# Written order on TensorE in the in-projection stage of a hybrid decoder step

## The chip, the cores and the metric

The kernel runs on one core of a Trainium2 chip. The metric is device time in microseconds, from one launch to its end; the time of a kernel is the median over its runs. PE is TensorE, DVE VectorE, ACT ScalarE, POOL GpSimd, SP SyncE.

## The reference, cut to what matters

One inference step of two trunk layers for 1024 prompt tokens and 64 sample tokens (8 requests of 8), all in float32. The stage that is changed is the in-projection of layer 0 and what follows it directly:

```
proj = x @ w_in                          # 1088 tokens, 1024 -> 2816
a = conformer_conv(proj[:, :512], proj[:, 512:1024])    # gate, 31 taps
xm = proj[:, 1024:] + mu * (prev - proj[:, 1024:])      # token shift
r, k, v, dw, da, dg = split(xm)
wlog  = -softplus(-(w0 + tanh(dw) @ w2)) - 0.5
decay = exp(-exp(wlog)) ;  a = sigmoid(a0 + da @ a2)
kk = k * k_k ;  kk = kk / max(sqrt(sum(kk * kk, head)), 1e-12)
kf = k * (1 + (a - 1) * k_a)
o, S = rwkv_scan(r, kf, v, decay, -kk, kk * a, state)   # 8 heads of 64
bonus = sum(r * kf * r_k, head) * v
```

The scan is computed in chunks of 64 tokens with masked products A of keys against queries and the inverse of a unit triangular matrix per chunk and head. After it come an output projection, a layer norm, a SwiGLU FFN, then layer 1 (pooling mixer and FFN).

## The kernel before, in words

Products in float32 are split in two parts each (`hl`, `xh`, `xl`), so each output tile of 128 features takes three products for each of the 8 slices k of the input. `proj` makes one tile: for three token blocks (384, 384, 320 tokens) 24 products into one psum buffer of the tag `mm` (two buffers), and then `evict`, which moves the block out on ACT and DVE. There are 22 tiles; `ORDER` gives their sequence:

```
ORDER = ("c0", "c1", 20, 21, 16, 12, 8, "c2", 17, 13, 9, "c3", 18, 14, 10, 19, 15, 11)
```

"c" tiles are the convolution (`conv_tile`: two tiles each, gate and value, and behind them 31 taps on DVE at line 319, of low priority, four small products on POOL and sums on DVE). 20 and 21 feed the small low-rank products. 16 + p, 12 + p and 8 + p are v, k and r of head pair p (`mix_tile`), p = 0 to 3.

`prep(p, blk, k)` prepares head pair p for token block blk. It is a Python generator: it issues its instructions up to a `yield`, and goes on at the next `next`. In order it makes: on PE the two low-rank products `pz` and `pa` (psum tag `o`, two buffers); tanh, scan `L`, exponentials `Wp` and `Wi`; on PE the sums of squares `pss` (psum tag `ch`); maximum `ri` on DVE (line 582), power on POOL (line 583), copy `exv` on ACT (line 586); on PE its transpose back (line 588) as a broadcast; `kn` on DVE (line 590), tanh `ta` on ACT (line 592), and on POOL `AR`, `kn`, `kf` and two parts of `BK` (lines 568 to 602). First `yield`. Then `AR` for r and the masked products `pA` on PE, two psum buffers for each of the two heads (tag `tp`, two buffers in all; `mm` for the last pair), which DVE masks into `ATm` (line 622), and the DMAs of all this to DRAM on SP's queue. Second `yield`. Then the bonus `pbn` and `bv`. `invert` inverts the diagonal blocks of a pair with 31 times two dependent instructions (lines 678 and 680), on POOL for pair 0 and the second part of pair 3, on DVE for the others. It loads its input back from DRAM.

Work is put on the engines by a planner: it takes instructions in the order of the program as priority, but plays the program through with modelled durations and gives each engine whatever is ready first. So the order of the queues of PE, ACT, DVE, POOL and SP around this stage is the planner's. From the second phase on (`phase2`, after the first part of the convolution's layer norm), `manual_schedule` takes that away for PE: PE's queue there is in the order in which the program is written.

After tile 12 + p the kernel before issues the first part of blocks 0 and 1, after tile 8 + p the second part of block 0, then block 2, block 1, block 2, the inversion and the third parts. With priority in program order these steps stand ahead of the tiles that follow.

Of the kernel before, what the change touches and what calls it, by code (L numbers as in the profile page):

```python
# [60 lines left out]
class Prog:  # L61
# [115 lines left out]

    GAP2 = 2.0

    _u = 0  # L180
    LATE = 2000
    CONV0 = 8
# [43 lines left out]
    def phase1(self):  # L226
        tc, nc, I, O = self.tc, self.nc, self.I, self.O
# [11 lines left out]
        es = ExitStack()  # L239
# [26 lines left out]
        def proj(m, evict):  # L266
            hl = first.pop(m, None) or self.load_w(I["w_in"][m].rearrange("p k f -> p (k f)"), f"in{m}")
            w = hl.rearrange("p s (k f) -> p s k f", k=KT)
            for b, (n0, n) in enumerate(NBLK):
                ps = self.psum("mm", f"in{m}_{b}")  # L270
                xh, xl = xb[b]
                for k in range(KT):
                    self.mm(ps[:, :n], w[:, 0, k, :], xh[:, k, :], k == 0, False)
                    self.mm(ps[:, :n], w[:, 0, k, :], xl[:, k, :], False, False)
                    self.mm(ps[:, :n], w[:, 1, k, :], xh[:, k, :], False, k == KT - 1)
                evict(b, n0, n, ps)

        self.accd = self.dr.tile([4, 128, TOK], F32, name="accd")
        def conv_tile(ct):
# [18 lines left out]
            def ev_val(b, n0, n, ps):  # L298
                for o, x in parts(n0, n, ps):
                    nc.vector.scalar_tensor_tensor(out=o, in0=o, scalar=1.0, in1=x, op0=ALU.add, op1=ALU.mult)  # L300

            proj(4 + ct, ev_gate)
            proj(ct, ev_val)
            nco = cvp.tile([128, (1 + NS) * CB], F32, tag="nco", name=f"nco{ct}")
            nc.scalar.activation(out=nco[:, 0:CB], in_=u[:, SEQ:SEQ + CB], func=AF.Copy, scale=0.5)
# [26 lines left out]
        def mix_tile(m):  # L332
# [16 lines left out]
            def ev(b, n0, n, ps):  # L349
# [5 lines left out]
                if p < n:  # L355
# [3 lines left out]
                                                   op0=ALU.mult, op1=ALU.add)  # L359

            proj(m, ev)
            sh = self.small.tile([128, 1 + NS], F32, tag="sho", name=f"sho{m}")
            nc.gpsimd.tensor_copy(out=sh[:, 0:1], in_=raw[:, SEQ:SEQ + 1])
# [7 lines left out]
            else:  # L371
                self.xm[m] = xm

        self.xm, done = {}, set()
        for x in self.ORDER:
            if isinstance(x, str):
                conv_tile(int(x[1]))
                continue
            mix_tile(x)
            done.add(x)  # L380
            p = x % 4
            if 16 <= x < 20:
                nc.scalar.dma_start(out=self.vd[p], in_=self.xm[x])
            elif 12 <= x < 16:
                jobs = [self.prep(p, blk, self.xm[x]) for blk in range(3)]
                next(jobs[0])
                next(jobs[1])
            elif 8 <= x < 12:
                next(jobs[0])
                if p == self.last_p:  # L390
                    self.invert(p, self.ip, 0, 6)
                for i in (2, 1, 2):
                    next(jobs[i])
                self.invert(p, self.ip, 6 if p == self.last_p else 0)
            if x in (16 + p, 8 + p) and {16 + p, 8 + p} <= done:
                for j in jobs:
                    next(j, None)
        es.close()


# [120 lines left out]
    def prep(self, p, blk, k):  # L521
# [9 lines left out]
        k = k[:, n0:n0 + n]  # L531
# [34 lines left out]
        def withW(out, in0, lo):  # L566

            nc.gpsimd.tensor_tensor(out=out[:, :cp], in0=ch(in0)[:, :cp], in1=Wv[:, :, lo:lo + 64], op=ALU.mult)
            if samp:
                nc.gpsimd.tensor_tensor(out=out[:, cp].rearrange("p (s l) -> p s l", l=8),  # L570
                                        in0=in0[:, np_:].rearrange("p (s l) -> p s l", l=8),
                                        in1=Ws[:, :, lo:lo + 8], op=ALU.mult)


        pss = self.psum("ch", f"pss_{nm}")
        prb = pss[:, 0:n]
# [7 lines left out]
        exv = self.tpool.tile([128, 6, 64], F32, tag="t", name=f"exv_{nm}")  # L584
        for a, b, m in ([(0, 6, 128)] if not samp else [(0, 4, 128), (4, 6, 64)]):
            nc.scalar.activation(out=exv[:m, a:b], in_=ri2[:m, a:b].unsqueeze(2).to_broadcast([m, b - a, 64]), func=AF.Copy, scale=-1.0)
        for i, (t0, m) in enumerate(TG):
            nc.tensor.transpose(prb[:, t0 - n0:t0 - n0 + m], exv[:m, 2 * i:2 * i + 2].rearrange("p a b -> p (a b)"), self.ident[:m, :m])
        kn = T("kn")
# [1163 lines left out]
```

## Time and profile before

| | us |
|---|---|
| median of 2 runs | 2301.02 (2300.99 to 2301.05) |
| the profiled execution | 2299.71 |
| its span, first to last instruction | 2297.9 |
| mean granted clock of TensorE, 1 is full speed | 0.953 |
| in-projection from its first product to its last | 7.5 to 401.3 |

The page of the profile gives for each engine the time in which it was busy. The span is that of the one core. A wait is told as the idle time of an engine before an instruction, with the instruction of another engine that ended it.

### The profile page before, as it was taken

The numbers are of one execution on the slowest core, as the hardware profiler recorded it, in microseconds if no ns is written. First come the engines' busy times: TensorE is split into PE (matmuls) and PEld (weight loads), VectorE is DVE, ScalarE is ACT, GpSimd is POOL, SyncE is SP. The second block draws the span as 40 slices with busy tenths as digits, with TensorE's granted clock in tenths as the row PEclk, the third lists the DMA queues.
The fourth block names the chain that finished last, engine by engine and source line by source line (L and its number), as shares of the span: only waits on it lengthen the run. The fifth ranks groups of instructions, "written<-read, shape, count | busy, mean of one in ns | idle before, by whom it ended". The sixth has DMA issues, their size and how long they took to land.

```text
span 2297.9 us, 39974 instructions
## 1 busy us (share of the span) xinstructions
PE 2148.6 (94%) x14794; PEld 1931.0 (84%) x14794; DVE 1672.4 (73%) x3115; ACT 906.4 (39%) x2031; POOL 445.6 (19%) x551
## 2 busy tenths in 40 slices
PE   8988899689888899999999999999999999999997
PEld 7887788467664699999998787879999999987876
DVE  6997798944457554888887767765388888877677
ACT  3242334545442543333333444443443333334452
POOL 3588966553421000000000001000000000000002
PEclk9999899598898899999999999999999999999999
DMA  5132334864541665666667785464386666678764
GB/s 171 42 104 91 109 89 132 235 187 117 159 133 57 215 236 196 224 222 221 221 211 255 255 281 174 140 197 146 133 284 224 228 220 222 204 261 274 241 195 136
DMA packets 286542, 427.68 MB, mean 186 GB/s; under 512 B 85484, under 2 KB 147844, under 8 KB 286339
## 3 DMA queue, kind: packets, MB, share of 16 engines
q1 hardware_dynamic: 209869, 318.44, 44.5%
q10 hardware_dynamic: 76478, 106.68, 13.2%
q8 instruction: 116, 1.90, 0.4%
q14 instruction: 79, 0.65, 0.1%
HBM read 296.14 MB, written 129.11 MB: 185 GB/s over the span
## 4 chain that ended last, share of the span: by engine, by line
PE 58%; DVE 6%; DMA 4%; issue 2%; ACT 2%; POOL 0%; SPq 0%; ACTq 0%; POOLq 0%; DVEq 0%
PE dn L74 14%; PE pp L74 1%; PE dr L74 1%; PE wo L74 1%; PE pl L74 1%; DMA yr<-yd 1%; ACT xo L155 1%; PE pa_1u L74 1%; PE pa_2u L74 1%; PE pa_4u L74 1%; PE pa_3g L74 1%; PE pa_5u L74 1%; PE pa_4g L74 1%; PE pa_2g L74 1%; PE pa_3u L74 1%
## 5 line engine op out<-in xcount | busy, mean ns | idle before, releaser
L74 PE MATMUL dn<-op_d,op_h 128*128 128x512 f32 x1848 | 452.6, 398 | 7.3 <-DVE yr L1297 3.7
L74 PEld LDWEIGHTS dn<-op_d,op_h 128*128 128x128 f32 x1848 | 346.0, 190 | 88.8 <-DVE yr L1297 5.2
L74 PE MATMUL in<-xh,hl_in 128*128 128x384 f32 (+1 forms) x1056 | 282.1, 348 | 15.9 <-ACT xh L71 7.5
L103 POOL TENSOR_TENSOR rstd_f<-rs_f,mhalf 128x1 f32<-128x1 f32 (+1 forms) x18 | 31.6, 1759 | 1343.1 <-DVE rs_f L102 689.6
L74 PEld LDWEIGHTS in<-xh,hl_in 128*128 128x128 f32 x1056 | 197.9, 199 | 29.2 <-ACT xm L352 7.8
L319 DVE SCALAR_TENSOR_TENSOR acc<-u,hv,acc 128x1024 f32<-128x1024 f32 x120 | 194.8, 1633 | 0.8
L74 PE MATMUL in<-xl,hl_in 128*128 128x384 f32 (+1 forms) x528 | 182.3, 345 | 2.2 <-DVE xl L95 2.2
L95 DVE TENSOR_TENSOR op_d<-raw_d,op_d 128x512 fp32r<-128x512 f32 x154 | 105.6, 686 | 62.3 <-ACT op_d L71 61.9
L71 ACT ACTIVATE op_d<-raw_d 128x512 fp32r<-128x512 f32 x154 | 96.2, 625 | 122.0 <-PE dn L74 89.5
L71 ACT ACTIVATE op_h<-ha 128x512 fp32r<-128x512 f32 x154 | 95.7, 624 | 84.3 <-PE dn L74 48.0
L95 DVE TENSOR_TENSOR op_h<-ha,op_h 128x512 fp32r<-128x512 f32 x154 | 105.0, 684 | 24.9 <-ACT op_h L71 24.7
L74 PEld LDWEIGHTS in<-xl,hl_in 128*128 128x128 f32 x528 | 104.6, 198 | 4.8 <-DVE xl L95 2.9
L155 ACT ACTIVATE xo<-xt,vec 128x128 f32<-128x128 f32 (+1 forms) x144 | 52.8, 456 | 45.7 <-PE xt L153 42.9
L74 PE MATMUL wo<-hl_woB,bhl 128*128 128x512 f32 (+1 forms) x216 | 66.5, 452 | 4.0 <-ACT bhl L71 3.5
L90 POOL TENSOR_TENSOR hl_in<-raw_in,hl_in 128x1024 fp32r<-128x1024 f32 x21 | 57.5, 2739 | 15.9 <-ACT hl_in L71 15.9
L74 PE MATMUL wo<-hl_woA,ahl 128*128 128x512 f32 (+1 forms) x216 | 56.0, 409 | 2.9 <-ACT hl_woA L71 1.6
L74 PEld LDWEIGHTS wo<-hl_woB,bhl 128*128 128x128 f32 (+1 forms) x216 | 41.7, 206 | 18.2 <-ACT bhl L71 4.7
L74 PEld LDWEIGHTS wo<-hl_woA,ahl 128*128 128x128 f32 (+1 forms) x216 | 39.3, 188 | 13.7 <-ACT hl_woA L71 1.8
L103 POOL TENSOR_TENSOR rstd_m<-rs_m,mhalf 128x1 f32<-128x1 f32 (+1 forms) x18 | 9.8, 544 | 196.8 <-DVE rs_m L102 196.8
L74 PE MATMUL dr<-op_d,hx 128*128 128x512 f32 (+1 forms) x132 | 40.3, 395 | 1.1 <-DVE hx L95 1.1
L71 ACT ACTIVATE rw<-in 128x384 f32<-128x384 f32 (+2 forms) x56 | 22.1, 394 | 47.1 <-PE in L74 31.8
L678 DVE TENSOR_TENSOR xt<-X,At 128x126 f32<-128x126 f32 (+33 forms) x93 | 33.5, 366 | 5.9 <-DMA X<-xinit 4.9
(1102 smaller groups left out, 5109.8 us busy)
## 6 DMA issues: line engine op xcount, KB each, us to landing
raw_t<-ffn_down SPq DMA_DIRECT2D x44, 512.0 KB
raw_d<-ffn_down SPq DMA_DIRECT2D x88, 256.0 KB
yr<-yd SPq DMA_DIRECT2D x30, 512.0 KB
raw_in<-w_in SPq DMA_DIRECT2D x22, 512.0 KB
xl<-xtd SPq DMA_DIRECT2D x16, 544.0 KB
ATm_t<-atd SPq DMA_DIRECT2D x16, 512.0 KB
xtd<-xo ACTq DMA_DIRECT2D x30, 256.0 KB
ha<-ha11d SPq DMA_DIRECT2D x22, 288.0 KB
```

The lines of the kernel that those rows point to most:

```text
L71: self.nc.scalar.activation(out=out, in_=in_, func=AF.Copy)
L74: self.nc.tensor.matmul(out, lhsT, rhs, start=start, stop=stop, **kw)
L90: (eng or nc.gpsimd).tensor_tensor(out=hl[:, 1, :], in0=raw, in1=hl[:, 0, :].bitcast(F32), op=ALU.subtract)
L95: (eng or self.nc.vector).tensor_tensor(out=out_lo, in0=src, in1=out_hi.bitcast(F32), op=ALU.subtract)
L103: nc.gpsimd.tensor_tensor(out=out, in0=t[:P, :n], in1=self.mhalf[:P, :n], op=ALU.pow)
L155: nc.scalar.activation(out=xo[:, k, :n], in_=ps[:, k * 128:k * 128 + n], func=AF.Identity, scale=self.v("lng", 16 * l + 4 * q + k), bias=s ...
L319: nc.vector.scalar_tensor_tensor(out=out, in0=src, scalar=cw(j), in1=out, op0=ALU.mult, op1=ALU.add)
L678: eng.tensor_tensor(out=xs, in0=X[:P, :m, s:s + 1].to_broadcast([P, m, w]), in1=At[:P, s:s + 1, s + 1:].to_broadcast([P, m, w]), op=ALU.mult)
```

## The change

The loop over `ORDER` now runs with PE's queue in written order. `prep` gets two more `yield`s, so that a token block has five steps: 0 low-rank products, tanh, scan and exponentials; 1 sums of squares, maximum, power, copy; 2 transpose back, `kn`, tanh, the POOL products; 3 masked products and outputs; 4 bonus. Steps are put on the list `side`, and `proj` takes one from it behind the products of k = 2, 5 and 7 of each block: nine slots per tile. After tile 12 + p six steps are put there (block.step): 0.0, 0.1, 1.0, 0.2, 1.1, 1.2. They go into the slots of tile 8 + p. After tile 8 + p come 0.3, 2.0, 2.1, 1.3, 2.2, 2.3, the inversion, and 0.4, 1.4, 2.4; these go into the nine slots of the next tile and the first of the one after. For the last pair there is no tile left, so its second list is issued behind the loop, where PE is planned again.

```
+    SLOTS = (2, 5, 7)
...
                     self.mm(ps[:, :n], w[:, 1, k, :], xh[:, k, :], False, k == KT - 1)
+                    if k in self.SLOTS and self.side:
+                        self.side.popleft()()
                 evict(b, n0, n, ps)
...
-        self.xm, done = {}, set()
+        self.xm = {}
+        man = ExitStack()
+        man.enter_context(tc.manual_schedule(engines={mybir.EngineType.PE}))
         for x in self.ORDER:
...
             elif 12 <= x < 16:
+                self.flush()
                 jobs = [self.prep(p, blk, self.xm[x]) for blk in range(3)]
-                next(jobs[0])
-                next(jobs[1])
+                self.side.extend(lambda j=jobs[i]: next(j) for i in (0, 0, 1, 0, 1, 1))
             elif 8 <= x < 12:
-                next(jobs[0])
+                self.flush()
+                self.side.extend(lambda j=jobs[i]: next(j) for i in (0,))
                 if p == self.last_p:
-                    self.invert(p, self.ip, 0, 6)
-                for i in (2, 1, 2):
-                    next(jobs[i])
-                self.invert(p, self.ip, 6 if p == self.last_p else 0)
-            if x in (16 + p, 8 + p) and {16 + p, 8 + p} <= done:
-                for j in jobs:
-                    next(j, None)
+                    self.side.append(lambda p=p: self.invert(p, self.ip, 0, 6))
+                self.side.extend(lambda j=jobs[i]: next(j) for i in (2, 2, 1, 2, 2))
+                self.side.append(lambda p=p: self.invert(p, self.ip, 6 if p == self.last_p else 0))
+                self.side.extend(lambda j=j: next(j, None) for j in jobs)
+        man.close()
+        self.flush()
...
+        yield
 
         pss = self.psum("ch", f"pss_{nm}")
...
             nc.scalar.activation(out=exv[:m, a:b], in_=ri2[:m, a:b].unsqueeze(2).to_broadcast([m, b - a, 64]), func=AF.Copy, scale=-1.0)
+        yield
```

## Rows read from the trace of the kernel before

**Rows 1.** Page, part 1: engine, busy us (share), instructions.

```profile
PE 2148.6 (94%) x14794; PEld 1931.0 (84%) x14794; DVE 1672.4 (73%) x3115; ACT 906.4 (39%) x2031; POOL 445.6 (19%) x551
```

**Rows 2.** By stage: stretch, length, busy PE, PEld, DVE, ACT, POOL, clock, DMA.

```profile
86.50:181.60 95.10, 84.73 (x465) 77.26 (x466) 83.23 (x84) 36.36 (x76) 66.38 (x64) 0.93 0.31 98
181.60:290.90 109.30, 90.09 (x474) 81.18 (x473) 82.28 (x79) 33.42 (x73) 96.83 (x123) 0.88 0.31 93
290.90:384.50 93.60, 86.22 (x476) 77.38 (x474) 93.08 (x131) 36.81 (x80) 68.60 (x66) 0.95 0.32 102
...
401.40:458.70 57.30, 35.20 (x148) 27.06 (x148) 55.29 (x159) 30.14 (x73) 29.48 (x40) 0.58 0.83 237
```

**Rows 3.** Waits of PE, 86.4 to 401.4: total us, times, longest.

```profile
PE pss_p1b L588 <- ACT exv_p1b L586: 9.2, 2, 7.9
PE in L74 <- ACT xm L352: 6.2, 3, 3.8
...
PE pz_p0b L74 <- ACT wa L367: 2.1, 1, 2.1
...
PE pA_p0b L74 <- POOL Wp_p0b L555: 0.2, 1, 0.2
```

**Rows 4.** Timeline of PE: start us, us, instruction; products, then a low-rank product.

```profile
64.84 0.52 PE L74 MATMUL in<-xh,hl_in 128*128 128x384 f32 x2
...
65.37 0.34 PE L74 MATMUL in<-xh,hl_in 128*128 128x384 f32 x1
...
209.56 0.91 PE L74 MATMUL pz_p1b<-wa,c_w2a 64*128 64x384 f32 x2
```

**Rows 5.** Timeline from 389 us: pair 3, block 0, from sum to POOL's last product.

```profile
389.00 0.83 PE L74 MATMUL pss_p3b<-c_hones,sq_p3b 128*128 128x2 f32 x6
...
393.49 0.52 ACT L586 ACTIVATE exv_p3b<-ri_p3b 128x384 f32<-128x384 f32 x1 [2.17 <-POOL ri_p3b L583]
...
395.40 0.49 PE L588 MATMUL pss_p3b<-ident,exv_p3b 128*128 128x128 f32 x3
...
401.77 1.05 POOL L601 TENSOR_TENSOR BK_p3b<-kn_p3b,s_p3b 128x384 f32<-128x384 f32 x1
```

**Rows 6.** Timeline from 208.9 us: pair 1, block 0, from sum to copy.

```profile
208.90 0.73 PE L74 MATMUL pss_p1b<-c_hones,sq_p1b 128*128 128x2 f32 x6
...
226.64 0.52 ACT L586 ACTIVATE exv_p1b<-ri_p1b 128x384 f32<-128x384 f32 x1 [12.56 <-POOL ri_p1b L583]
...
227.90 0.58 ACT L592 ACTIVATE ta_p1b<-pa_p1b,hv 128x384 f32<-128x384 f32 x1
```

**Rows 7.** Timeline from 164.5 us: pair 0, block 2, from broadcast to BK's copy.

```profile
164.57 0.27 PE L588 MATMUL pss_p0b<-ident,exv_p0b 64*128 64x64 f32 x1
...
174.50 0.47 ACT L71 ACTIVATE BK_p0b<-BK_p0b 128x320 f32<-128x320 f32 x1 [2.49 <-POOL BK_p0b L601]
```

**Rows 8.** Timeline from 402.9 us: masked products, the first mask, the next products.

```profile
402.88 1.60 PE L74 MATMUL pA_p3b<-AR_p3b,BK_p3b 64*128 64x128 f32 x12
...
409.22 0.68 DVE L622 TENSOR_TENSOR ATm_p3b<-pA_p3b,c_maskP 128x512 f32<-128x512 f32 x1
...
409.95 2.93 PE L74 MATMUL pA_p3b<-AR_p3b,BK_p3b 64*128 64x128 f32 x12 [3.53 <-DVE ATm_p3b L622]
```

**Rows 9.** Groups, 86.4 to 401.4: taps (busy us, mean ns); then POOL's timeline.

```profile
L319 DVE SCALAR_TENSOR_TENSOR acc<-u,hv,acc 128x1024 f32<-128x1024 f32 x97 | 153.7, 1594 | 0.5
```
```profile
256.63 2.00 POOL L600 TENSOR_TENSOR qq_p1b<-xm,qq_p1b 128x384 f32<-128x384 f32 x1
...
398.36 1.03 POOL L600 TENSOR_TENSOR qq_p3b<-xm,qq_p3b 128x384 f32<-128x384 f32 x1 [0.79 <-ACT qq_p3b L593]
```

**Rows 10.** By stretch, `xt` (inversion) alone; then PE's timeline, pair 3, block 1.

```profile
401.40:428.20 26.80, 0.00 (x0) 0.00 (x0) 15.05 (x42) 0.00 (x0) 0.00 (x0) 0.61 0.81 237
428.20:445.60 17.40, 0.00 (x0) 0.00 (x0) 9.70 (x40) 0.00 (x0) 0.00 (x0) 0.50 0.97 287
```
```profile
412.81 0.90 PE L588 MATMUL pss_p3b<-ident,exv_p3b 128*128 128x128 f32 x3
```

More of the change, by code (lines that the diff above doesn't have):

```diff
@@ L379, in phase1 @@
             mix_tile(x)
-            done.add(x)
             p = x % 4
@@ L384, in phase1 @@
             elif 12 <= x < 16:
+                self.flush()
                 jobs = [self.prep(p, blk, self.xm[x]) for blk in range(3)]
-                next(jobs[0])
-                next(jobs[1])
+                self.side.extend(lambda j=jobs[i]: next(j) for i in (0, 0, 1, 0, 1, 1))
             elif 8 <= x < 12:
-                next(jobs[0])
+                self.flush()
+                self.side.extend(lambda j=jobs[i]: next(j) for i in (0,))
                 if p == self.last_p:
-                    self.invert(p, self.ip, 0, 6)
-                for i in (2, 1, 2):
-                    next(jobs[i])
-                self.invert(p, self.ip, 6 if p == self.last_p else 0)
-            if x in (16 + p, 8 + p) and {16 + p, 8 + p} <= done:
-                for j in jobs:
-                    next(j, None)
+                    self.side.append(lambda p=p: self.invert(p, self.ip, 0, 6))
[4 more added lines that the diff above has]
+        self.flush()
+        es.close()
         es.close()
```

## The prediction

> **What bounds the kernel now.** I read four views, from coarse to fine. The page first: PE is busy for 2148.6 us of the 2297.9 us span [rows 1], so what can be won is PE's idle time and the time it runs at the lower clock. The table by stage comes second [rows 2]. The change touches the 314.9 us from 86.5 to 401.4, and through them the 57.3 us up to 458.7, in which the last head pair is prepared. In the first three rows PE is busy 84.73 of 95.10, 90.09 of 109.30 and 86.22 of 93.60 us, with a granted clock of 0.93, 0.88 and 0.95 (1 is 2.4 GHz, 0.5 is 1.2 GHz); DVE is busy 83, 82 and 93 us there, POOL 66, 97 and 69. So PE leads this stage, but no other engine is far behind. In the last row PE falls to 35.20 of 57.30 us at clock 0.58 while DVE is busy for 55.29: the tail belongs to DVE. The third view says what PE waits for up to 401.4 [rows 3]: eleven groups, from 9.2 us down to 0.2, 36.9 us together. Some 30 us of the 36.9 are steps of the preparation waiting for ACT, POOL or DVE, 6.2 are products waiting for a psum buffer to be evicted. The fourth view, the timeline, gives the lengths of the chains behind these waits.
>
> **What the change does to them.** The planner now may not reorder TensorE in this stage. Before, it put a step of the preparation behind as many products as it thought the step's inputs needed. After, step and products follow each other as written: a slot after product rows k = 2, 5 and 7 of each token block, one step in each. Products, transposes and vector work are the same in number; nothing is removed or added but order and waits. What counts is the cover: the PE work that stands between a step and the next of the same block. Three products take 0.53 us [rows 4], so slots are 1.6, 1.06 and 1.6 us of products apart (three, two, three rows of k). I name step s of block b as b.s, counted from 0.
>
> *0.1 to 0.2 (sum of squares to its broadcast).* Between them stand 1.06 + 1.6 us of products and the two matmuls of 1.0 at 0.91 us each [rows 4]: 4.5 us. The chain is sum on PE, maximum on DVE, power on POOL, copy on ACT. Its shortest run is from 389.83 (389.00 + 0.83) to 394.01, 4.2 us, with POOL idle; its longest from 209.63 to 227.16, 17.5 us, with POOL in the inversion of pair 0 [rows 5, 6]. That inversion now is issued in the middle of tile c2 and should be nearly over when pair 1 is prepared, so I take 7, nearer to the short end. Wait 2.5 us (0 to 5: the matmul of 1.0 needs the psum buffer that 0's tanh releases, and that tanh ran right behind the copy [rows 6], so the wait may move forward to where cover is thinner).
>
> *1.1 to 1.2.* They stand in neighbouring slots: cover 1.06 us. Wait 7 - 1.06 = 6 us (3.1 to 9).
>
> *2.2 to 2.3 (broadcast to the masked products).* Again neighbours, 1.06 us. The chain is one DVE product and five POOL products: from 395.89 to 402.82, 6.9 us, in one case, from 164.84 to 174.97, 10.1 us, in another [rows 5, 7]. I take 8. Wait 7 us (5.9 to 9).
>
> *Inside each step 3.* The second head's products need the psum buffer of the first's, which DVE empties by the mask (0.68 us). The planner put other products between; where it had none, PE stood 3.53 us [rows 8]. In written order there never are any. Half a tap of the convolution (mean 1.594 us [rows 9]) in front of the mask, the mask, less the first head's second bank (a third of the 1.60 us): 0.8 + 0.7 - 0.5 = 1.0 us, 3.0 per pair (1 to 10).
>
> The other distances (0.2 to 0.3, 1.2 to 1.3, 2.1 to 2.2, the bonus) have 6 to 15 us of cover against the same chains; they cost nothing while that cover lasts, and 3 to 9 us each if a long chain like that of rows 6 comes back.
>
> The sum for one pair is 2.5 + 6 + 7 + 3 = 18.5 us, for pairs 0 to 2 it is 55.5. Pair 3 makes only its first six steps inside the stage: 8.5. The waits for eviction stay (6.2): a step in the slot k = 7 is issued ahead of its block's eviction, hidden by the next block (24 products, 4.2 us). The 2.1 us for a matmul that the planner had hoisted ahead of its input go [rows 3]. After: 55.5 + 8.5 + 6.2 = 70.2 us against 36.9, **+33 us**. The clock I leave as it is: more waits, but shorter ones than the longest of 7.9 [rows 3]; bounds -4 to +8.
>
> The moved steps also issue their DMAs: on SP two weight-cut columns, the outputs and the diagonal blocks, eight or so per step 3, and bv on ACT's queue. SP also brings the weights of the tiles to come, and an instruction that waits for its chain holds them up. Two weight buffers, some 24 us of products, cover this, and in rows 3 PE never waits for weights: nothing. Without the cover it would be PE's wait for the rest of the chain again.
>
> **The tail** gets shorter. Pair 2's inversion ran on DVE here: 15.05 us up to 428.2, and about half of the 9.70 up to 445.6, where pair 3's first part joins it [rows 10]. Its last masks now come in the sixth slot of tile 19, two tiles before the end, so most of it moves forward into time when DVE's convolutions are done. And 1.1 and 1.2 of pair 3, which ended at 413.71 [rows 10], now lie before the last product. DVE was busy for 96% of the tail, so taking 20 us from it helps, unless the chain of pair 3 itself or the landing of its blocks sets the end: between 0 and -24, I take **-15**.
>
> **Sum.** +33 - 15 = +18 us. The profiled execution took 2299.71 us, 1.8 more than its span and 1.3 less than the median 2301.02, so the forecast by the median is **2319 us**, 0.8% slower. A change under 2% (46 us) can hardly be told from none here.
>
> **Rivals.**
> *It gets faster: the waits are short because the others have caught up.* While PE waits, DVE, POOL and ACT empty their queues, and the next chain runs at its shortest. Then 1.1 to 1.2 costs 3.1, 2.2 to 2.3 costs 5.9, step 3 3.0, 0.1 to 0.2 nothing: 12 us a pair, 36 for three, 3 for pair 3, 4 for evictions, 43 in all, +6; the tail gives -20 and the clock -4: 2283. For it: DVE has 12 and 27 us of idle time in the first two rows of rows 2, POOL 29, 12 and 25 in the three, and pair 1's chain loses its inversion. Against it: DVE's idle time is filled with convolution taps as soon as there are any. It decides when the waits add up to less than about 52 us.
>
> *It gets slower by more than 2%: the chains stay as long as when the engines are busy.* 1.1 to 1.2 costs 9, 2.2 to 2.3 costs 9, step 3 6, 0.1 to 0.2 4: 28 a pair, 84, with 13 for pair 3 and 6 for evictions 103, +66; the tail gives only -10: 2357. For it: the same POOL product of 128x384 took 2.00 us with taps on DVE and 1.03 us without [rows 9], and a wait of PE is just when the planner gives DVE a tap. Beside this stands a rule of the Trainium skill, SBUF — State Buffer, section "Who interferes with whom": a VectorE instruction with two SBUF inputs and a GpSimd instruction that reads SBUF shut each other out for a whole instruction. By that rule, five POOL products at 2.00 us make the chain of 2.2 to 2.3 10.6 us, and PE's waits would not shorten it while taps are left.
>
> *It does not do what it says:* if ACT, DVE and POOL keep their old order, PE arrives at every step when it did before. Then 2301, within 5. Rows 3 speak against it: PE waited there for some 30 us although the planner had put products ahead of each step, and the written order puts fewer.
>
> **How the numbers follow.** Forecast 0.47 (its own range 2302 to 2338), faster rival 0.30, slower rival 0.15, no effect 0.08. The range that leaves out no more than 2 in 10 reaches from the faster rival, a little beyond its price, to the price of the slower: 2279 to 2357. Over 2% faster needs waits near zero and the whole tail: 0.05. Over 2% slower (above 2347) is the upper part of the slower rival and some of the unknown cost of step 3: 0.15. Within 2%: 0.80.
>
> **What would show it.** Right: the view of PE's waits puts the broadcast behind ACT's copy and the masked products behind POOL at three to eight us each, in every pair; a new group of masked products waiting for DVE's mask; the last product of the stage at about 430; pair 2's inversion done before it; the tail under 50 us. Wrong: the same waits summing to under 50 us (faster), or over 90 (slower); the tail as long as before, if pair 3's own chain sets it. The step that I trust least is the length that the three chains will have, since the order on ACT, DVE and POOL is planned anew.

## The result, and the profile after

The changed kernel took 2360.93 us (2358.94 to 2362.92) against 2301.02: a ratio of 1.030, interval 1.0255 to 1.0344. The forecast was 2319, with 2357 as the upper end. The profiled execution's span went from 2297.9 to 2361.1 us, by 63.2. The page after, part 1 (engine, busy us, instructions), answers to [rows 1]:

```profile
PE 2161.9 (92%) x14794; PEld 1942.9 (82%) x14794; DVE 1664.6 (71%) x3115; ACT 908.2 (38%) x2031; POOL 444.8 (19%) x551
```

The number of instructions is the same on every engine; PE is busy 13.3 us longer for them and idle for 49.9 us more. Where that is, the table by stage says (length, busy PE, PEld, DVE, ACT, POOL, clock, DMA). After, the three stretches of [rows 2], then the whole stage, then the tail up to the first output product and from there to the first state product (`pc_t`) of the next stage:

```profile
86.60:205.30 118.70, 94.50 (x476) 85.41 (x476) 80.33 (x86) 37.97 (x80) 75.30 (x87) 0.83 0.29 92
205.30:328.40 123.10, 89.91 (x474) 82.07 (x474) 83.46 (x107) 34.07 (x73) 90.04 (x103) 0.82 0.28 85
328.40:437.00 108.60, 82.02 (x399) 74.16 (x398) 84.86 (x111) 33.62 (x72) 62.80 (x60) 0.78 0.26 77
...
86.60:475.20 388.60, 300.40 (x1521) 271.83 (x1520) 277.24 (x383) 122.40 (x259) 244.58 (x272) 0.82 0.28 84
...
475.20:515.50 40.30, 27.27 (x114) 21.06 (x113) 28.87 (x80) 18.69 (x47) 18.63 (x29) 0.56 0.87 277
515.50:579.50 64.00, 53.21 (x260) 39.53 (x260) 32.73 (x72) 28.65 (x68) 34.14 (x73) 0.77 0.62 175
```

Before, the whole stage in one row:

```profile
86.60:401.40 314.80, 277.94 (x1509) 250.54 (x1510) 265.49 (x316) 116.76 (x253) 239.12 (x264) 0.92 0.33 100
```

A stretch less PE's busy time is its waits: 388.6 - 300.4 = 88.2 us after, 314.8 - 277.9 = 36.9 before. So of the 73.8 us that the stage got longer, 51.3 are waits and 22.5 are PE's work at a lower clock (0.82 for 0.92; by estimate 2 us of it are 12 instructions more, mostly of pair 3, that now lie inside the stage). DVE and POOL are busy for a smaller share of the longer stage (DVE 71% for 84%, POOL 63% for 76%): they wait as well. In the tail the first output product comes 40.3 us behind the last product, for 57.3 before; but the first state product comes 104.3 us behind it, for 105.5 before. What the tail won, it gave back at once. Behind that point the changed kernel was 9.5 us shorter, and 73.8 - 1.2 - 9.5 = 63.1, the 63.2 of the spans but for rounding. The 9.5 us say nothing on the change: the same unchanged part took 1781.6 us here and 1767.5 us in a second profile of the same kernel (`c_after` below).

The view of PE's waits after (total us, times, longest), stage only, answers to [rows 3]:

```profile
PE pa_p1b L74 <- ACT s_p1b L550: 18.6, 1, 18.6
PE in L74 <- ACT xm L355: 8.0, 4, 3.5
PE pa_p2b L74 <- ACT s_p2b L550: 7.4, 1, 7.4
PE pa_p0b L74 <- ACT s_p0b L550: 6.2, 1, 6.2
PE pss_p2b L595 <- ACT exv_p2b L592: 5.9, 1, 5.9
PE pss_p0b L595 <- ACT exv_p0b L592: 5.5, 1, 5.5
...
PE pA_p2b L74 <- DVE ATm_p2b L629: 5.4, 3, 4.7
PE pA_p2b L74 <- POOL BK_p2b L608: 4.4, 1, 4.4
```

The longest is new: 18.6 us in front of pair 1's second low-rank product in step 1.0. Its timeline is read from the end backwards, an engine at a time (start us, us, instruction, in brackets the idle time and what ended it):

```profile
235.85 0.47 PE L74 MATMUL pss_p1b<-c_hones,sq_p1b 128*128 128x2 f32 x3
...
256.88 1.65 PE L74 MATMUL pa_p1b<-wa,c_w2a 64*128 64x384 f32 x2 [18.55 <-ACT s_p1b L550]
...
255.84 0.52 ACT L592 ACTIVATE exv_p1b<-ri_p1b 128x384 f32<-128x384 f32 x1 [8.92 <-POOL ri_p1b L589]
256.27 0.56 ACT L550 ACTIVATE s_p1b<-pz_p1b,hv 128x384 f32<-128x384 f32 x1
...
241.45 2.59 DVE L322 SCALAR_TENSOR_TENSOR acc<-u,hv,acc 128x1024 f32<-128x1024 f32 x2
243.96 1.14 DVE L553 TENSOR_TENSOR_SCAN L_p1b<-c_scan,s_p1b 128x384 f32<-128x384 f32 x1
245.02 0.13 DVE L588 TENSOR_SCALAR ri_p1b<-pss_p1b 128x6 f32<-128x6 f32 x1
...
254.25 0.26 POOL L687 TENSOR_TENSOR X<-X,xt 128x30 f32<-128x30 f32 x1
254.47 1.34 POOL L589 TENSOR_TENSOR ri_p1b<-ri_p1b,mhalf 128x6 f32<-128x6 f32 x1
```

`pa` of block 1 needs the psum buffer that block 1's tanh `s` empties. That tanh stands in ACT's queue behind block 0's copy `exv`, which waits for POOL's power, which stands in pair 0's inversion (its `X` steps run up to 256), and which waits for the maximum `ri` on DVE, 0.13 us long, behind taps, the token shift and the scan. PE's sums had ended at 236.32: 8.7 us passed in DVE's queue and 9.3 in POOL's. A product that needs nothing of this chain but a free buffer pays for all of it, and behind it every product of the tiles.

### The profile page after: what moved, and what is told of

Its sections match the earlier page's. It is cut to its first block, busy times and chain, and to the rows that moved or that the text cites. A ratio compares the mean times of both kernels' runs of the same rounds, so it can differ in the third digit from the quotient of the medians.

```text
span 2361.1 us, 39989 instructions
## 1 busy us (share of the span) xinstructions
PE 2161.9 (92%) x14794; PEld 1942.9 (82%) x14794; DVE 1664.6 (71%) x3115; ACT 908.2 (38%) x2031; POOL 444.8 (19%) x551
## 4 chain that ended last, share of the span: by engine, by line
PE 54%; DVE 5%; DMA 5%; ACT 2%; issue 2%; SPq 0%; POOL 0%; ACTq 0%; POOLq 0%; DVEq 0%
PE dn L74 14%; PE dr L74 1%; PE pp L74 1%; DMA xl<-xtd 1%; PE wo L74 1%; PE pl L74 1%; DMA yr<-yd 1%; ACT xo L155 1%; PE pa_3u L74 1%; PE pa_4g L74 1%; PE pa_4u L74 1%; PE pa_5u L74 1%; PE pa_5g L74 1%; PE pc_10g L74 1%; PE pb_9u L74 1%
## 5 line engine op out<-in xcount | busy, mean ns | idle before, releaser
L74 PE MATMUL dn<-op_d,op_h 128*128 128x512 f32 x1848 | 447.2, 394 | 7.0 <-DVE yr L1304 3.3
L74 PEld LDWEIGHTS dn<-op_d,op_h 128*128 128x128 f32 x1848 | 342.6, 188 | 87.4 <-DVE yr L1304 3.8
L74 PE MATMUL in<-xh,hl_in 128*128 128x384 f32 (+1 forms) x1056 | 299.4, 360 | 20.6 <-ACT xm L355 8.0
L74 PEld LDWEIGHTS in<-xh,hl_in 128*128 128x128 f32 x1056 | 208.1, 208 | 34.3 <-issue 10.4
L74 PEld LDWEIGHTS in<-xl,hl_in 128*128 128x128 f32 x528 | 110.0, 208 | 3.8 <-DVE xl L95 2.8
L74 PE MATMUL wo<-hl_woA,ahl 128*128 128x512 f32 (+1 forms) x216 | 65.1, 449 | 7.7 <-ACT hl_woA L71 6.7
L71 ACT ACTIVATE hl_in<-raw_in 128x1024 fp32r<-128x1024 f32 x22 | 23.4, 1065 | 41.7 <-PE in L74 39.0
## 6 DMA issues: line engine op xcount, KB each, us to landing
raw_d<-ffn_down SPq DMA_DIRECT2D x88, 256.0 KB
xtd<-xo ACTq DMA_DIRECT2D x30, 256.0 KB
```

Of the source, the lines that this page charges most:

```text
L71: self.nc.scalar.activation(out=out, in_=in_, func=AF.Copy)
L74: self.nc.tensor.matmul(out, lhsT, rhs, start=start, stop=stop, **kw)
```

## The experiments

One row for each kernel: ratio to the kernel before on the same chip, then from its profile the end of the last in-projection product, PE's waits and PE's busy time from 86.6 us to there. Each expectation uses its own letters for its theories.

| kernel | ratio (interval) | last product | waits | PE busy |
|---|---|---|---|---|
| before (its profile) | 1 | 401.4 | 36.9 | 277.9 |
| changed (its profile) | 1.0300 (1.0255, 1.0344) | 475.2 | 88.2 | 300.4 |
| c_after | 1.0283 (1.0242, 1.0324) | 479.2 | 91.1 | 301.5 |
| e1_planned | 0.9998 (0.9978, 1.0018) | 404.0 | 35.7 | 281.7 |
| e11_all_planned | 0.9981 (0.9950, 1.0012) | 394.8 | 32.0 | 276.2 |
| e2_inv0_dve | 1.0295 (1.0258, 1.0332) | 476.8 | 91.0 | 299.2 |
| e3_first_list | 1.0284 (1.0250, 1.0318) | 461.5 | 83.7 | 291.2 |
| e4_second_list | 1.0264 (1.0223, 1.0305) | 460.9 | 80.5 | 293.8 |
| e5_all | 1.0171 (1.0121, 1.0221) | 444.5 | 66.2 | 291.7 |
| e6_spread | 1.0252 (1.0211, 1.0292) | 463.5 | 89.0 | 287.9 |
| e7_lowlow | 1.0337 (1.0287, 1.0387) | 497.2 | 85.2 | 325.4 |
| e8_all_spread | 1.0280 (1.0217, 1.0343) | 456.6 | 78.6 | 291.4 |
| e12_all_apart | 1.0222 (1.0173, 1.0270) | 447.7 | 70.1 | 291.1 |
| e15_heads_apart | 1.0161 (1.0114, 1.0208) | 431.7 | 59.4 | 285.8 |
| e10_inv_late | 1.0617 (1.0562, 1.0673) | 456.8 | 73.8 | 296.5 |
| e9_one_tap | 0.9967 (0.9942, 0.9993) | 398.5 | 35.5 | 276.4 |
| b_one_tap | 0.9700 (0.9655, 0.9745) | 342.6 | 0.0 | 256.0 |
| e13_half_taps | 1.0367 (1.0329, 1.0405) | 490.7 | 98.3 | 305.8 |
| e14_half_taps_planned | 0.9993 (0.9970, 1.0016) | 398.8 | 33.1 | 279.1 |
| e16_no_inv3 | 1.0244 (1.0202, 1.0285) | 472.0 | 88.9 | 296.5 |

**Is it the written order?** e1 keeps the five steps, lists and slots, and gives PE's order back to the planner:

```
-        man.enter_context(tc.manual_schedule(engines={mybir.EngineType.PE}))
```

> Steps, slots and lists as in the changed kernel, but TensorE's queue is planned again, as before. Theory A (the written order itself makes PE stand at each chain of another engine): the planner puts products ahead of late steps again, the waits of 88 us fall to about 40 and the time to 2295 to 2315. Rival B (the loss comes from where the steps are now issued, because ACT, DVE and POOL are planned by that): the time stays at 2345 to 2365.

0.9998, and waits of 35.7 us for 36.9 before: theory A. Where the steps are issued in the program costs nothing that can be told; this written order is the whole loss.

**Three single edits.** e2 takes pair 0's inversion from POOL to DVE, e3 orders the first list so that each step is followed by the other block's, e4 draws two bonus steps in between 2.2 and 2.3; c_after is the level on the second chip.

```
-    PINV = ((0, 0), (3, 6), (None, 0))                 # e2
+    PINV = ((3, 6), (None, 0))
-    ... for i in (0, 0, 1, 0, 1, 1))                   # e3
+    ... for i in (0, 1, 0, 1, 0, 1))
-    ... for i in (2, 2, 1, 2, 2))                      # e4
+    ... for i in (2, 2, 1, 2, 0, 1, 2))
```

> The changed kernel with pair 0's inversion on DVE instead of POOL. Theory A with its sub-cause (pair 1's matmul of step 1.0 waits 18.6 us because POOL's power for block 0 is queued among the inversion): that wait falls to some 7 us as in pairs 0 and 2, the time by 11 us of wait and 4 us of clock, to about 2346. Rival (the wait is DVE's lateness with scan and maximum, 8 of the 18.6 us): it stays above 14 us and the time at 2355 to 2365, as DVE gets more work.

> The changed kernel with the first list in the order 0.0, 1.0, 0.1, 1.1, 0.2, 1.2. Theory A (step 1.0 pays for the chain of 0.1, since the tanh that frees its psum buffer stands behind block 0's copy in ACT's queue): the waits at 1.0 (34.3 us in all) vanish, those before both transposes come to about 5 us a pair and 12 in pair 1, in all 22 against 53; with the clock 2318 to 2330. Rival B (issue places): the waits move to the transposes in full, 2350 to 2365.

> The changed kernel with the bonus steps of blocks 0 and 1 between 2.2 and 2.3. Theory A: cover grows from 1.06 to about 6 us, the three waits of masked products for POOL (12.6 us in all) go to under 3, the time by them and 4 us of clock to about 2346. Rival (the chain is late by POOL's queue, whatever stands between): waits stay over 9 us and the time within 5 us of 2361.

> The changed kernel once more, unaltered, as the level for the three others on this chip. Both theories: 1.030 of the kernel before (1.025 to 1.034).

Each alone stays within the interval of the changed kernel, so none gained the 15 us or more of its theory A, though each took away the wait it aimed at. In e2 pair 1's wait for `s` fell to 6.9 us, and its masked products then waited:

```profile
PE pA_p1b L74 <- DVE ATm_p1b L629: 10.7, 3, 10.0
...
PE pa_p1b L74 <- ACT s_p1b L550: 6.9, 1, 6.9
```

In e3 the wait for `s` went and the broadcast, which needs the same `exv`, took its place:

```profile
PE pss_p1b L595 <- ACT exv_p1b L592: 17.8, 1, 17.8
```

In e4 the waits of masked products for POOL fell from 12.6 to 1.3 us as theory A said, and those for the masks in pairs 0 to 2 rose from 10.0 to 15.0.

**All three, with and without the planner.** e5 has the three edits, e11 the same under the planner.

> Pair 0's inversion on DVE, the first list as 0.0 1.0 0.1 1.1 0.2 1.2 and 0.4 and 1.4 drawn in between 2.2 and 2.3, all at once. Theory A (the waits of TensorE in a pair add up to the length of its chains less the PE work between the first step and the last; a new order only moves them): waits of the stage again 75 to 90 us, ratio 1.020 to 1.028, that is no more than the second list alone gave (1.026). Rival B (the three edits take away three separate waits, which the earlier single edits each moved to one of the other two places): waits under 60 us, ratio 1.012 or less.

> The three edits together with TensorE's order left to the planner again. Theory A (the written order is the whole cost, and lists matter only under it): ratio 0.996 to 1.004. Rival F (the edits have a worth of their own, the inversion on DVE above all): ratio below 0.996 or above 1.004.

e5 gains 1.1 percentage points on c_after, and their intervals don't meet; alone the three gained -0.1, 0.0 and 0.2. With one place taken away the wait moved to another, with all three it got shorter. That lies between the two theories, nearer to rival B: waits of 66 us, not under 60, and 1.017, not 1.012. Under the planner the edits change nothing that can be told.

**Distance.** e6 leaves slots empty, three in the first list and two after each step of the second (pairs 0 and 1). e7 puts products of the two low parts in front of each step. e8 is e5 with three empty slots between 1.1 and 0.2 and two after each step of the second list. e12 is e5 with the empty slots in the second list alone, four of them ahead of 0.3. e15 is like e12, with the two heads of step 3 in slots of their own and the empty slots placed anew around them.

```
-    ... for i in (0, 0, 1, 0, 1, 1))
+    ... for i in (0, 0, None, 1, 0, None, 1, None, 1))               # e6, None: no step
+    for kk in {2: (0, 1, 2), 5: (3, 4, 5), 7: (6, 7)}[k]:            # e7, before a step
+        self.mm(ps[:, :n], w[:, 1, kk, :], xl[:, kk, :], False, False)
+    for f, gap in zip(steps, (4, 1, 0, 2, 2, 1, 1, 2, 0, 2)):        # e12, pairs 0 and 1
+        self.side.extend([lambda: None] * gap + [f])
+            if hd == 0:                                              # e15, in prep's step 3
+                yield
```

> The same steps in the same order, but spread: the first list takes all nine slots of its tile (three slots without a step), and for pairs 0 and 1 each step of the second list is followed by two slots without a step, so that it fills three tiles instead of one. Theory A (waits = chains less cover): the two second lists get 18 empty slots of 1.4 us each, 25 us a pair, against waits of some 15 to 25 us in them; the waits of the stage fall from 88 to about 55 us, the granted clock rises with it and PE's busy time falls by some 8; 30 to 40 us less than the changed kernel, ratio 1.013 to 1.018. Rival C (the chains grow as they are drawn apart, because DVE and POOL fill the time with convolution and inversion): waits stay above 78, ratio 1.025 or more.

> At each slot that has a step, the product of the two low parts is added for the rows since the last slot: two or three products more per step, some 144 in all, 25 us of PE at 0.177 us each. The output stays within what the reference asks. Theory A (the chains set the time, the products are only cover): the waits fall by about as much as the products add, 88 to about 65 us, and the time stays within 8 us of the changed kernel (ratio 1.027 to 1.034), or falls a little if the clock stays up longer. Rival D (PE's own work is the bound and the waits stand at the steps however much lies between): 25 us more, ratio 1.041.

> The three edits together (ratio 1.017, waits of the stage 66 us) and drawn apart: three slots without a step between the first list's sums and its broadcasts, and for pairs 0 and 1 two after each step of the second list. Theory A (distance helps where a step waits for the step before it of the same block, nowhere else): the masked products' waits for POOL in pairs 0 and 1 (5.6 and 5.9 us) lose 2.8 us each or more, pair 2's broadcast waits (4.8) go, the waits for the masks inside a step (3.5, 7.0 and 9.1) stay: 66 to about 54 us, ratio 1.010 to 1.014. Rival C (chains grow as they are drawn apart): waits 63 us or more, ratio 1.016 or more.

> The three edits together, with the first list as there (six neighbouring slots) and only the second list of pairs 0 and 1 drawn apart: four slots without a step ahead of 0.3, two ahead of 1.3 and of 2.2, and two between 1.4 and 2.3, with single ones between. In the spread kernel before, 0.2 and 0.3 had come to stand closer (two slots in place of five), and just that wait grew (5.6 to 14.3 us in pair 0). Theory A (distance counts where the wait is): the masked products' waits for POOL in pairs 0 and 1 (5.6, 5.9 us) fall under 2 each, the stage's waits 66 to about 55, ratio 1.008 to 1.016. Rival C (chains grow as they are drawn apart): waits 64 us or more, ratio 1.017 or more.

> As the kernel with the second lists drawn apart (ratio 1.022, waits 70 us, of which 13.0 and 13.8 for the masks in pairs 0 and 1), and the masked products of a block's two heads are steps of their own there, with one slot without a step between the heads (0.3, 1.3, 2.3 in pairs 0 and 1). Theory A (distance counts where the wait is, and the masks are the last place): the masks' waits in pairs 0 and 1 fall to about 6 together, the stage's waits to about 52, ratio 1.010 to 1.017. Rival J (the waits belong to the order on DVE, which runs its taps where the planner put them, and only change their place): waits 62 us or more, ratio 1.019 or more.

e6 fell to rival C: waits 89.0. Most of them stand in the first list, where it had added little. e7 fell between: its ratio lies in A's range, and its interval leaves out D's 1.041, but its trace speaks against A: 145 products more, PE 325.4 - 300.4 = 25.0 us busier, and only 3 us less of waits (6 against c_after) in place of 23, so the stage took 18 to 22 us more.

```profile
86.60:497.20 410.60, 325.41 (x1666) 298.63 (x1665) 274.13 (x383) 123.80 (x259) 245.67 (x272) 0.83 0.26 80
```

In e8 I had moved 0.2 to the end of its list and so next to 0.3, two slots ahead of it in place of five. That wait grew most, from 5.6 us in e5 (pair 1: 5.9):

```profile
PE pA_p0b L74 <- POOL BK_p0b L613: 14.3, 1, 14.3
PE pA_p1b L74 <- POOL BK_p1b L613: 11.5, 1, 11.5
```

e12 put it right: pairs 0 and 1 no longer waited for POOL. But the masks inside the step took over (3.5 and 7.0 us in e5), and the sum stayed:

```profile
PE pA_p1b L74 <- DVE ATm_p1b L634: 13.8, 3, 5.3
PE pA_p0b L74 <- DVE ATm_p0b L634: 13.0, 3, 7.7
```

With a slot between the heads, e15, these fell too, to 9.4 and 5.4:

```profile
PE pA_p1b L74 <- DVE ATm_p1b L638: 9.4, 3, 5.8
...
PE pA_p0b L74 <- DVE ATm_p0b L638: 5.4, 2, 4.8
```

The stage's waits, 59.4 us, lie between the two theories' ranges, the ratio in theory A's; but e5 and e15 can't be told apart by their times. In these runs distance helped at the very step that waited, and by less than its length. No written order with all its taps came nearer to the kernel before than 1.6%.

**What fills the queues.** e10 issues the inversions of pairs 0 to 2 behind the stage. e9 leaves out 30 of the 31 taps on DVE, and b_one_tap does the same to the kernel before. e13 and e14 cut each tap in two of half the columns, in the changed kernel and in the one before.

```
-                for j in range(CONVW):
+                for j in range(1):                                   # e9, b_one_tap
+                for j, h in ((j, h) for j in range(CONVW) for h in (0, SEQ // 2)):   # e13, e14
```

> The changed kernel with the inversions of pairs 0, 1 and 2 issued behind the last product of the stage instead of inside it. Rival E: pair 1's wait in the second block's gates falls from 18.5 to about 7 us, as it did with that inversion on DVE, and no other wait grows in its place: waits of the stage 88 to about 70 us. Theory A: DVE's taps fill what the inversions leave, pair 1 loses some 10 us and the others nothing: 75 to 82. By both the tail grows by 20 to 50 us, and the ratio is 1.03 to 1.05; what counts is when the last product ends.

> The changed kernel with one of the 31 taps of each convolution tile on DVE (the convolution's result for the long sequence is left out, some 150 us of DVE in the stage). Theory A (half of the chains' length is time in DVE's queue behind taps): waits of the stage 88 to about 55 us, the stage ends 40 us earlier, and the tail shortens too, ratio below 1.010. Rival E (POOL sets the chains: its inversion for pair 1, its five products for the masked products): pair 1's wait in the second block's gates stays at 15 us or more, waits 75 us or more, the stage ends less than 20 us earlier.

> The kernel before (planner's order) with one of the 31 taps of each convolution tile on DVE; the convolution's result for the long sequence is left out. Theory A (taps in DVE's queue cost the written order its waits, while the planner hides its own): the stage's waits fall little, 37 to 25 or more, the last product of the stage ends at 385 to 400 us, and the ratio is 0.985 to 0.998, near the written order's with one tap (0.997). Rival G (the taps cost both orders alike): waits near zero, the last product before 350 us, ratio below 0.975.

> The changed kernel with every DVE tap of 1024 columns as two of 512, the same work in pieces of half the length. Theory A (each DVE step of a chain stands behind the rest of one tap, so PE's waits go with the length of one piece): waits of the stage 88 to about 65 us, ratio 1.015 to 1.024. Rival H (the amount of taps ahead counts, several in a row as at 241 to 244 us in pair 1, not the length of one): waits 80 us or more, ratio 1.027 or more.

> The kernel before with the same half taps. Theory A: the planner's order already hides most of it; ratio 0.992 to 1.003. Rival: the smaller pieces cost more on DVE than they free, above 1.003, or they free as much as in the written order, below 0.992.

e10: pair 1's wait fell to 7.4 us as rival E said, the waits to 73.8, between the two theories' ranges; the three inversions then cost far more behind the stage than expected (the first state product came 189 us behind the last product, for 104: 85 us more, not 20 to 50). e9 looked like the proof that the taps are the cause: the stage as short as before the change. Its control took that back. The table by stage, e9 and then b_one_tap:

```profile
86.60:398.50 311.90, 276.41 (x1505) 252.10 (x1503) 134.35 (x279) 117.67 (x249) 173.45 (x261) 0.91 0.33 98
```
```profile
86.60:342.60 256.00, 256.00 (x1505) 232.84 (x1503) 109.03 (x226) 114.59 (x244) 171.30 (x259) 1.00 0.39 118
```

With one tap of 31 the planner's order has not one wait and the full clock. The written order costs 55.9 us of the stage there, 35.5 of waits and 20.4 of clock, against 73.8, 51.3 and 22.5 with taps; over the whole kernel 0.9967 / 0.9700 = 1.028 (two kernels on two chips, about 1.022 to 1.033), as much as with them. So rival G holds, and e9 alone would have misled: three quarters of the stage's loss are there without the taps, which add 16 us of waits to 35 and cost either order some 3% of the whole. e13 was no clean test: the half taps kept DVE busy for 183.7 us in place of 150.2. The planner hid that (0.9993), the written order did not (waits 98.3).

**The tail.** e16 leaves out the 31 steps of pair 3's inversions.

```
-        for s in range(31):
+        for s in range(0 if p == self.last_p else 31):
```

> The changed kernel without the 31 steps of both inversions of pair 3 (the inverse of pair 3's blocks is left out; its loads and stores stay). Theory K (pair 3's chain sets the tail: blocks, inversion, their way back): the time from the last product to the first state product falls from 104 to 85 us or less, the whole by 15 us or more, ratio 1.023 or less. Rival L (the stretch is set by its transfers, 22.3 MB in 105 us, or by the output products with their weights): 98 us or more, ratio 1.026 or more.

From the last product to the first state product it took 562.6 - 472.0 = 90.6 us, between the two. By that pair 3's inversion is worth some 13 us of the 104; what sets the other 90 was not found. In the other kernels with their inversions in place it was 96 to 111 us, with all taps or one, planned or written, and the interval of e16's ratio meets that of c_after, so a gain in the whole time is not shown.

## Why the prediction was wrong

The way was right: slower, by waits at the steps that were named, with a shorter stretch up to the first output product. Three terms of the sum were wrong: step 1.0 by 24.3 us, the clock by 22.5, the tail by 13.8. The other waits came out 6.3 us below their prices. With the 9.5 us behind the tail, which the change did not make, that is 24.3 - 6.3 + 22.5 + 13.8 - 9.5 = 44.8 of the 45 us by which the spans' 63.2 missed the forecast's 18.

| term | predicted | measured |
|---|---|---|
| step 1.0, priced as 0.1 to 0.2 (buffer of `pa`) | 2.5 a pair, 10.0 | 34.3 |
| 1.1 to 1.2 (`pss` for `exv`) | 24.0 | 18.9 |
| 2.2 to 2.3 (`pA` for `BK`) | 21.0 | 12.6 |
| masks inside step 3 | 9.0 | 10.0 |
| evictions (`xm`, `sdg`) | 6.2 | 10.9 |
| sums for `sq` | 0 | 1.5 |
| waits in all, less the 36.9 of before | +33 | +51.3 |
| clock | 0 | +22.5 |
| tail | -15 | -17 at the first output product, -1.2 at the first state product |

**First, the clock**, left as it was for "more waits, but shorter ones", with bounds of -4 to +8. Shorter waits cost it as well. In e9 the longest is 4.4 us. Its table by stretch: 11 us of products, the wait, the products behind it:

```profile
196.00:207.26 11.26, 11.26 (x66) 9.60 (x64) 2.60 (x6) 6.09 (x13) 10.01 (x25) 1.00 0.17 48
207.26:211.70 4.44, 0.00 (x0) 0.00 (x0) 1.16 (x1) 1.26 (x4) 4.21 (x9) 0.99 0.38 119
211.70:216.00 4.30, 4.30 (x10) 3.22 (x11) 0.96 (x1) 3.21 (x7) 0.82 (x2) 0.50 0.42 65
216.00:222.00 6.00, 5.09 (x26) 4.67 (x25) 0.78 (x2) 1.34 (x3) 4.10 (x4) 0.80 0.35 110
```

PE was busy without a break at 1.00 (2.4 GHz), stood 4.44 us, and found 0.50 (1.2 GHz) behind it. After, a wait of 2.10 us in pair 3 did the same:

```profile
437.00:456.80 19.80, 19.79 (x112) 17.80 (x110) 17.26 (x53) 7.52 (x17) 3.94 (x9) 1.00 0.24 81
456.80:458.90 2.10, 0.01 (x1) 0.01 (x1) 1.93 (x8) 1.74 (x5) 1.27 (x2) 1.00 0.04 1
458.90:462.90 4.00, 4.00 (x11) 3.19 (x12) 3.15 (x9) 2.35 (x5) 0.84 (x2) 0.57 0.00 0
```

Not every wait does. In the traces of before, changed, c_after, e5, e9 and e15 all 39 waits of 3 us or more that began at full clock found a lower one behind them (a mean under 0.9 in the next 3 us), and some 30 of the 80 shorter ones. b_one_tap, without waits, needs 256.0 us for the stage's products, the small ones of the preparation included, all at 1.00. Against that the kernel before lost 21.9 us to the clock for 36.9 us of waits, e9 20.4 for 35.5, e15 29.8 for 59.4, the changed kernel 44.4 for 88.2: in these four each microsecond of waits cost another 0.5 to 0.6 (0.36 to 0.72 in the others). Forecast waits of +33 would so have cost some 17 more, and the sum would have been near 2336. The Trainium skill, TensorE: Matmul & The Clock Gate, section HAM oscillation — how this bites in real kernels, tells of a kernel that loses its full clock again at each wait for data; these rows agree.

**Second, step 1.0.** I had seen that its `pa` hangs on the buffer that a tanh behind the copy releases (by the trace it is block 1's own `s`, not a tanh of block 0), and still priced it with the chain of 0.1 to 0.2 and its cover of 4.5 us. Ahead of `pa` stand only 1.06 us of products and `pz`, 0.91: by the prediction's own 7 us that is a wait of 5, by the 17.5 of [rows 6] one of 15.5. And it took the short end, since pair 0's inversion "should be nearly over". It ran on POOL from 195.0 to 256.3, and in pair 1 the chain took from 236.32 to 256.88, 20.6 us. In pairs 0 and 2, without it, the wait was 6.2 and 7.4. e2 and e10, where the wait was 6.9 and 7.4, show that the inversion made 11 us of the 18.6.

**Third, the tail.** The first output product came 17 us sooner, for the reason given; but the step from there to the whole was not shown by any row, and the first state product did not follow it.

Of the other terms, 1.1 to 1.2 and 2.2 to 2.3 were too dear by 13.5 us together, the evictions too cheap by 4.7. The faster rival's chains at their shortest, 43 us, are near to what the same order waited with one tap, 35.5, by the sum and not by the parts: 10.3 of the 35.5 stand at step 1.0, which it put at nothing. That rival then fell with its clock of -4 and with chains that did not stay short. The forecast also held that under 2% can hardly be told from none; the interval of the result, 0.9% wide, would have told its 0.8%.

The slower rival came out by its size, 2357 for 2360.93, and not by its mechanism. Its POOL products at 2.00 us hardly occurred: of the 11 products of line 607 in the stage one came near. Those of pair 1, after and in e9 (shortest, median, longest in ns):

```profile
L607 POOL TENSOR_TENSOR qq_p1b<-xm,qq_p1b x3: 858/1347/1971, 264.6 to 300.5; 128x384 f32<-128x384 f32 x2, 128x320 f32<-128x320 f32 x1
```
```profile
L607 POOL TENSOR_TENSOR qq_p1b<-xm,qq_p1b x3: 862/1017/1021, 218.8 to 245.6; 128x384 f32<-128x384 f32 x2, 128x320 f32<-128x320 f32 x1
```

And the wait for `BK` at 2.2 to 2.3, which this rival put at 9 us, was 3.9, 4.3 and 4.4 us with the taps and 3.9, 4.4 and 4.4 without. What the taps did lengthen is pair 0's inversion. Its 62 steps on POOL, after and in e9 (stretch, length, busy POOL, clock, DMA):

```profile
86.60:300.00 213.40, 39.11 (x62) 0.82 0.26 80
```
```profile
86.60:300.00 213.40, 24.93 (x62) 0.92 0.34 103
```

By these 14.2 us the queue in which pair 1's power stands is longer. The rule of the Trainium skill that stood beside this rival, SBUF — State Buffer, section Who interferes with whom, agrees with these steps and with the single product of 1.97 us; in the waits for `BK` it does not show.

**What stays open:** why distance shortened the waits by less than its length. The likeliest reason is that DVE's order is still the planner's, so that more distance is filled with more taps ahead of the chain's next step; whether a written order for DVE too would keep the taps out of the chains was not tried. Nor was the planner's own order of PE, fixed as a written one: so it is not shown whether any fixed order could do as well as the planner's, or whether fixing it has a price of its own.

## What to carry to other kernels

Before an engine's order is written by hand, hold each distance between two dependent steps against the length of the chain between them, counted through every queue that the chain crosses. Count the buffers that a step needs, too, since a buffer released late holds up a product that has no other tie to the chain. Price the waits of TensorE with the clock that they cost, here about half a microsecond more for each, and do so for waits of 4 us as for long ones. When an experiment that lightens a load makes the loss go away, lighten it in the kernel before as well: here the written order cost 2.8% with one tap and 2.8 to 3.0% with all.

## What the hardware showed beyond expectation

The stage's some 1510 matrix instructions took 256.0 us at full clock and 301.5 us in c_after, about 2 of them for products that lie inside the stage only there: some 14% of TensorE's busy time is clock alone. Cutting a tap of 1024 columns (mean 1559 ns) in two of 512 (mean 981 ns) made DVE's taps 22% dearer, 183.7 us for 150.2. And the 62 steps of an inversion on POOL took 39.1 us beside DVE's taps and 24.9 us with one tap of 31.
